# A transformer block pair on one core: quarter sums of weights by accumulating DMAs in DRAM, norm weights on the activations, seven products for the conv's output

## The chip, the core and the metric

The kernel runs on one core of a Trainium2 chip. The metric is the device time of one execution in microseconds: 2034.69 us, the median of three runs (2034.37 to 2036.16). A row such as L242 names line 242 of the kernel before; PE is TensorE, DVE VectorE, ACT ScalarE, POOL GpSimd, SP SyncE, whose queue carries the loads.

## What is computed

512 tokens of width 1024, all in fp32, in two blocks one behind the other.

```python
def first_block(x, ...):
    xn = rmsnorm(x, norm1_g)
    qa, ka, va, qr, kr, vr, gr, gate_a, gate_b = split(xn @ w_in)
    # dilated window attention (3 groups of 4 heads), retention (4 heads), gates, projections
    x = x + mix @ w_out
    return x + relu(rmsnorm(x, norm2_g) @ w_up) ** 2 @ w_down      # 1024 -> 4096 -> 1024
def second_block(x, ...):
    h = rmsnorm(x, a_norm)
    b, c, u, z = split(h @ a_w_in)                                  # 1024 -> 4 x 2048
    y = b * conv3(c * u) * silu(z)                                  # causal, 3 taps
    x = x + y @ a_w_out                                             # 2048 -> 1024
    # shared keys and values, then compressed, selected and window attention
    return rmsnorm(x, final_norm)
```

The rmsnorm is x / sqrt(mean(x^2) + 1e-6) * g; g are the norm weights.

## The kernel before

Every product is made of fp32r halves: each operand is split into hi (rounded, by ACT) and lo (the rest, by DVE), and `mm3` (L241 to L244) issues three matmuls, hi hi, hi lo and lo hi. A unit of weights is 512 rows by 512 columns, 1 MB; it costs 48 matmuls of 512 columns for all tokens. `Weights` (L42 to L158) keeps a list of all units in order: `get` (L151) hands out one, starts the load of the unit two further on (SP's queue, two raw buffers of 512 KB) and splits the next one. A unit without a norm weight is split in pieces of 128x1024 (ACT L127, DVE L128); one with a norm weight in four times as many instructions of 128x512, since the weight g goes with the row (ACT L131, DVE L132).

`gemm` (L267) takes two units of 1024 rows and accumulates four banks. With `halves` it takes the tokens 0 to 255 first and then 256 to 511, so that it can start when half of the activations are there.

The FFN's second product, `down(q)` (L808), is done by `gemm7` (L246) for each quarter q of the 4096: the quarter of activations and the 1024x1024 of weights are cut in 2 x 2 and multiplied with seven products instead of eight (Strassen's scheme, in Winograd's form). It needs sums of the activation parts (s1 to s4) and of the weight parts (t1 to t4). The weight parts w11, w12, w21, w22 are loaded, and DVE adds them in place between the splits (L118; splits L113, L114). The activation sums are made when `up` evacuates: ACT and DVE split them (`operand`, L765 and L766), DVE makes s1 (L793) and POOL s2, s3, s4 (L796, L797, L799). One product of `gemm7` is 24 matmuls of 512 columns (2 token tiles x 4 x 3). The order is p1 p5 p2 p3 p7 p6 p4; DVE adds the banks to the residual (L815), in the last quarter POOL adds u = p1 to six places of it.

At the end of the last `down` the rows are normed (`norm`, L226: ACT squares, DVE takes one-element steps L206 to L214 for the inverse root, and scales to xs, L235), transposed by PE (`split_T`, L216, PE L221) and split (ACT L223, DVE L224); then the conv's first `gemm` starts, in halves. The conv: `conv_blocks(j)` (L875), j = 0 to 3, makes 512 channels each in four `gemm`s c, u, z, b; `conv_out(j, cb)` (L923) multiplies them with a_w_out in plain products of 48 matmuls, 8 of them, and DVE adds half of the result to the residual (L929). Behind the last one the four tokens are normed and transposed one by one, for the keys and values of the attention (`kc_run`, L990, again in halves). The order of the jobs is that of the program; between products, generators of attention and retention issue their steps.

## Time and profile before

| | |
|---|---|
| median of 3 runs | 2034.69 us (2034.37 to 2036.16) |
| profiled execution | 2032.5 us, its span 2030.7 us |
| PE busy | 1981.3 us, 98% of the span, 9836 instructions |
| DVE busy | 1215.2 us, 60% |
| ACT busy | 912.8 us, 45% |
| POOL busy | 214.9 us, 11% |
| DMA | 185.75 MB, mean 91 GB/s |

Busy time is the sum over an engine's instructions. The profile's waits tell what released an engine that had been idle; its windows give busy time, granted clock and the share of the DMA engines for a stretch of the span.

### The profile page before, as it was taken

Reading aid. Unit: us, or ns where it says so; the run is one execution under the profiler, and the core shown is the slowest. Engines: PE = TensorE matmul, PEld = TensorE weight load, DVE = VectorE, ACT = ScalarE, POOL = GpSimd, SP = SyncE. Lnnn points to the kernel's source line nnn. Section 1 sums busy time; section 2 is a strip of 40 time slices with the busy share of each in tenths; the row PEclk is TensorE's granted clock in tenths of the full one; section 3 lists DMA queues with packets and bytes.
Section 4 is the critical chain, followed back from the end, with each engine's and each line's share of the span. In section 5 each row is a group of like instructions: output and inputs, shape, how many; then the busy total and the mean of one; then the engine's idle time right before and its main releaser. Section 6 shows DMA issues by size and latency. Waiting matters only on the chain. (4 is left out here: it accounts for less than half of the span.)

```text
span 2030.7 us, 25768 instructions
## 1 busy us (share of the span) xinstructions
PE 1981.3 (98%) x9836; PEld 1642.8 (81%) x9836; DVE 1215.2 (60%) x2183; ACT 912.8 (45%) x1723; POOL 214.9 (11%) x276
## 2 busy tenths in 40 slices
PE   8999999999999999999999899999999999999997
PEld 6888887888888888888888688888888898787776
DVE  6464456464555664486876955344435645769777
ACT  5454443333424233564453443333233334677776
POOL 0000001000000000011010301010101001315452
PEclk9999999999999999999999999999999999999999
DMA  4424322322223233413313133332332352210111
GB/s 152 145 68 125 95 68 84 102 70 88 84 88 94 79 96 127 157 62 124 114 63 125 31 94 91 97 103 84 104 104 83 124 164 84 63 52 28 67 32 42
DMA packets 104363, 185.75 MB, mean 91 GB/s; under 512 B 6896, under 2 KB 27920, under 8 KB 103984
## 3 DMA queue, kind: packets, MB, share of 16 engines
q1 hardware_dynamic: 99920, 172.51, 27.5%
q10 hardware_dynamic: 3264, 7.30, 1.0%
q0 software_dynamic: 1056, 4.29, 0.6%
q8 instruction: 77, 1.26, 0.3%
q14 instruction: 46, 0.38, 0.1%
HBM read 177.74 MB, written 6.34 MB: 91 GB/s over the span
## 5 line engine op out<-in xcount | busy, mean ns | idle before, releaser
L132 DVE SCALAR_TENSOR_TENSOR wl<-raw,vec,wh 128x512 fp32r<-128x512 f32 (+2 forms) x480 | 332.8, 730 | 311.8 <-ACT wh L131 300.7
L244 PE MATMUL g<-xh,wl 128*128 128x512 f32 (+1 forms) x1280 | 479.8, 375 | 2.9 <-DVE wl L132 2.9
L242 PE MATMUL g<-xh,wh 128*128 128x512 f32 (+1 forms) x1280 | 481.7, 377 | 0.6 <-ACT xh L223 0.6
L243 PE MATMUL g<-xl,wh 128*128 128x512 f32 (+1 forms) x1280 | 478.5, 374 | 0.0
L131 ACT ACTIVATE wh<-raw,vec 128x512 fp32r<-128x512 f32 (+2 forms) x480 | 309.4, 690 | 371.4 <-PE g L243 217.9
L244 PEld LDWEIGHTS g<-xh,wl 128*128 128x128 f32 x1280 | 241.5, 189 | 46.8 <-DVE wl L132 4.2
L242 PEld LDWEIGHTS g<-xh,wh 128*128 128x128 f32 x1280 | 241.5, 189 | 42.4 <-ACT xh L223 1.2
L243 PEld LDWEIGHTS g<-xl,wh 128*128 128x128 f32 x1280 | 241.7, 189 | 41.7 <-DVE xl L224 0.2
L242 PE MATMUL g<-wh,xh 128*128 128x512 f32 x512 | 204.4, 400 | 0.4 <-ACT wh L131 0.4
L243 PE MATMUL g<-wl,xh 128*128 128x512 f32 x512 | 201.4, 393 | 0.3 <-DVE wl L132 0.3
L244 PE MATMUL g<-wh,xl 128*128 128x512 f32 x512 | 200.7, 392 | 0.0
L242 PEld LDWEIGHTS g<-wh,xh 128*128 128x128 f32 x512 | 96.7, 189 | 20.1 <-ACT wh L131 1.1
L244 PEld LDWEIGHTS g<-wh,xl 128*128 128x128 f32 x512 | 96.4, 188 | 20.2 <-DVE xl L224 0.3
L243 PEld LDWEIGHTS g<-wl,xh 128*128 128x128 f32 x512 | 96.7, 189 | 18.8 <-DVE wl L132 0.7
L128 DVE TENSOR_TENSOR wl<-raw,wh 128x1024 fp32r<-128x1024 f32 x44 | 53.9, 1224 | 78.2 <-ACT wh L127 76.9
L127 ACT ACTIVATE wh<-raw 128x1024 fp32r<-128x1024 f32 (+1 forms) x60 | 56.5, 944 | 95.2 <-PE g L244 58.1
L796 POOL TENSOR_TENSOR s<-s,r 128x512 f32<-128x512 f32 x8 | 13.5, 1685 | 767.1 <-DVE s L793 767.1
L113 ACT ACTIVATE wh<-w 128x1024 fp32r<-128x1024 f32 x56 | 58.9, 1057 | 65.9 <-PE g L244 58.7
L114 DVE TENSOR_TENSOR wl<-w,wh 128x1024 fp32r<-128x1024 f32 x56 | 71.0, 1279 | 23.7 <-ACT wh L113 23.5
L1340 POOL TENSOR_TENSOR p<-p,ad 128x512 f32<-128x512 f32 (+3 forms) x96 | 68.3, 740 | 102.3 <-DVE ad L1335 97.8
L1328 ACT ACTIVATE p<-ps,am 128x512 f32<-128x512 f32 (+3 forms) x128 | 66.2, 529 | 22.4 <-DVE am L1326 17.1
L1326 DVE TENSOR_REDUCE am<-ps 128x1 f32<-128x512 f32 (+3 forms) x88 | 53.6, 637 | 17.3 <-PE ps L1324 16.4
(353 smaller groups left out, 3448.6 us busy)
## 6 DMA issues: line engine op xcount, KB each, us to landing
raw<-in_w_in SPq DMA_DIRECT2D x84, 512.0 KB, 3.6
raw<-in_a_w_in SPq DMA_DIRECT2D x64, 512.0 KB, 3.9
raw<-in_w_up SPq DMA_DIRECT2D x32, 512.0 KB, 4.0
w<-in_w_down SPq DMA_DIRECT2D x32, 512.0 KB, 4.2
raw<-in_w_in SPq DMA_DIRECT2D x32, 256.0 KB, 3.2
raw<-in_w_proj_b SPq DMA_DIRECT2D x16, 512.0 KB, 3.7
raw<-in_a_w_out SPq DMA_DIRECT2D x16, 512.0 KB, 3.9
raw<-in_b_w_in SPq DMA_DIRECT2D x16, 512.0 KB, 3.8
```

The costliest lines, as they stand in the source:

```text
L113: nc.scalar.activation(wh, raw, AF.Copy)
L114: nc.vector.tensor_sub(wl, raw, wh.bitcast(F32))
L127: nc.scalar.activation(wh[:, k], raw[:, k], AF.Copy)
L128: self.sub.tensor_sub(wl[:, k], raw[:, k], wh[:, k].bitcast(F32))
L131: nc.scalar.activation(wh[:, k], raw[:, k], AF.Copy, scale=gk)
L132: nc.vector.scalar_tensor_tensor(wl[:, k], raw[:, k], gk, wh[:, k].bitcast(F32), op0=ALU.mult, op1=ALU.subtract)
L242: PE.matmul(ps, lh, rh, start=start, stop=False, skip_group_check=not check)
L243: PE.matmul(ps, lh, rl, start=False, stop=False, skip_group_check=not check)
L244: PE.matmul(ps, ll, rh, start=False, stop=stop, skip_group_check=not check)
L1326: V.tensor_reduce(m[:, h0:h0 + hp], ps, axis=AX.X, op=ALU.max, negate=True)
L1328: A.activation(p[:, h], ps[:, h], AF.Exp, bias=m[:, h0 + h:h0 + h + 1], accum_out=d[:, h0 + h:h0 + h + 1])
L1340: G.tensor_tensor(pp[h], pp[h], d[:, h:h + 1].to_broadcast([P, n]), op=ALU.mult)
```

## The change

Five things are done together.

- Quarter sums. t1 to t4 of the four `down` quarters and of the two 1024x1024 blocks of a_w_out are formed in DRAM: POOL issues a copy DMA of a quarter and then a DMA that adds another quarter to it. For each of the six blocks these are four copies and four adds of 1 MB, 48 DMAs in all. They are issued four at a time, behind a one-column copy on POOL that reads a result of the retention's q/k, gate and v products (`sum_some`). The seven units of a block are then loaded like any others.
- Raw buffers are four instead of two until the attention stage begins.
- The norm weights of norm1, norm2 and anorm are multiplied onto the activations in `split_T` (eight pieces of 128x128 a token tile, each with its scale), so that the units of w_in, w_up and a_w_in are split in pieces of 128x1024. Two norms keep theirs on the weights.
- `gemm7` runs in the order p1 p7 p4 p5 p6 p2 p3; all activation sums are made on DVE, s3 with a11 in the first pass. In the last block, tokens 256 to 511 are normed after p6 and tokens 0 to 255 after p3; the next `gemm` takes the half of tokens 256 to 511 first, then come the transposes of the others (`late`), then the other half.
- The conv's output product is two `gemm7`s, one before the b product of block 2 and one at the end. The factor 0.5 goes into the taps.

The diff, cut to its core:

```diff
-    ORDER = ("w11", "t1", "w21", "w22", "t3", "t2", "t4")
...
+    def raws_in(self, pool, bufs):
+        while self.raws:
+            self._split()
+        self.raw_pool, self.raw_bufs = pool, bufs
...
-            raw = self.pool.tile([128, 1024], F32, tag="raw", name="raw", bufs=2)
+            raw = self.raw_pool.tile([128, 1024], F32, tag="raw", name="raw", bufs=self.raw_bufs)
...
-        if isinstance(raws, str):
-            for raw in self.q[self.PLACE.get(raws, raws)]:
-                wh, wl = self._halves(2, 512)
-                nc.scalar.activation(wh, raw, AF.Copy)
-                nc.vector.tensor_sub(wl, raw, wh.bitcast(F32))
-                out += [(wh[:, k], wl[:, k]) for k in range(2)]
-            for a, b in self.SUMS.get(raws, ()):
-                for x, y in zip(self.q[a], self.q[b]):
-                    nc.vector.tensor_tensor(x, x, y, op=ALU.add)
-            self.ready.append(out)
-            return
...
-    def split_T(dst_h, dst_l, t, src):
+    def split_T(dst_h, dst_l, t, src, gain=None):
         for b in range(2):
             ps = psa.tile([P, 4, P], F32, tag="tr", name="tr", bufs=2)
             for k in range(4):
                 PE.transpose(ps[:, k], src[:, (4 * b + k) * P:(4 * b + k + 1) * P], ident)
             oh = dst_h[:, 4 * b:4 * b + 4, t * P:(t + 1) * P]
-            A.activation(oh, ps, AF.Copy)
-            V.tensor_sub(dst_l[:, 4 * b:4 * b + 4, t * P:(t + 1) * P], ps, oh.bitcast(F32))
+            ol = dst_l[:, 4 * b:4 * b + 4, t * P:(t + 1) * P]
+            if gain is None:
+                A.activation(oh, ps, AF.Copy)
+                V.tensor_sub(ol, ps, oh.bitcast(F32))
+            else:
+                for k in range(4):
+                    gk = vcol(gain, 4 * b + k, 4 * b + k + 1)
+                    A.activation(oh[:, k], ps[:, k], AF.Copy, scale=gk)
+                    V.scalar_tensor_tensor(ol[:, k], ps[:, k], gk, oh[:, k].bitcast(F32),
+                                           op0=ALU.mult, op1=ALU.subtract)
...
+    late = []
+    def arrive(t, xs, gain=None):
+        x = cur["x"]
+        if t < 2:
+            late.append(lambda: split_T(*x, t, xs, gain))
+        else:
+            split_T(*x, t, xs, gain)
...
-        for name, o, base in (("p1", "a11", None), ("p5", "s1", None), ("p2", "a12", "p1"), ("p3", "s4", "p5"),
-                              ("p7", "s3", None), ("p6", "s2", None), ("p4", "a22", "p7")):
+        for name, o, at_ in (("p1", "a11", "g0"), ("p7", "s3", "g1"), ("p4", "a22", "g1"), ("p5", "s1", "os"),
+                             ("p6", "s2", "g1"), ("p2", "a12", "g0"), ("p3", "s4", "os")):
             w = ws.get()
-            bb = banks[name] = banks[base] if base else [psg.tile([P, 512], F32, tag="g", name="g") for _ in range(2)]
+            new = name in ("p1", "p7", "p5", "p6")
+            if new:
+                banks[at_] = [psa.tile([P, 512], F32, tag=at_[i], name="g") if at_ == "os" else
+                              psg.tile([P, 512], F32, tag="g", name="g") for i in range(2)]
...
+    def st_unit(w, k0, c0, sums):
+        d = {f"w{a + 1}{b + 1}": (w, k0 + 512 * a, 4, [(c0 + 512 * b, 512)], None) for a in range(2) for b in range(2)}
+        d.update({n: (sums[n], 0, 4, [(0, 512)], None) for n in sums})
+        return [d[n] for n in ("w11", "t3", "t4", "t1", "t2", "w21", "w22")]
+    def st_sums(w, k0, c0):
+        q = {(a, b): w[k0 + 512 * a:k0 + 512 * a + 512, c0 + 512 * b:c0 + 512 * b + 512]
+             for a in range(2) for b in range(2)}
+        t = {n: dr.tile([512, 512], F32, name=f"{n}_{len(st_names)}") for n in ("t1", "t2", "t3", "t4")}
+        st_names.append(0)
+        def put(n, src):
+            return lambda: G.dma_start(out=t[n], in_=src)
+        def add(n, src):
+            return lambda: G.dma_start(out=t[n], in_=src, accum_op=ALU.add)
+        return t, [put("t1", q[0, 0]), put("t3", q[0, 1]), add("t1", q[0, 1]), add("t3", q[1, 1]),
+                   put("t2", t["t1"]), add("t2", q[1, 1]), put("t4", t["t2"]), add("t4", q[1, 0])]
+    def operands(make, hold, first, h, r0, r1, scratch):
+        def put(name, src):
+            if h == 0:
+                hold[name] = [make(name, x) for x in "hl"]
+            hi, lo = (x[:, 2 * h:2 * h + 2] for x in hold[name])
+            A.activation(hi, src, AF.Copy)
+            V.tensor_sub(lo, src, hi.bitcast(F32))
+        a11, a21 = r0[:, :, 0:256], r0[:, :, 256:512]
+        if first:
+            put("a11", a11)
+            s3 = scratch()
+            V.tensor_sub(s3, a11, a21)
+            put("s3", s3)
+            return
+        a12, a22 = r1[:, :, 0:256], r1[:, :, 256:512]
+        s1, s2 = scratch(), scratch()
+        put("a22", a22)
+        V.tensor_sub(s1, a21, a22)
+        put("s1", s1)
+        V.tensor_sub(s2, s1, a11)
+        put("s2", s2)
+        put("a12", a12)
+        V.tensor_tensor(s2, s2, a12, op=ALU.add)
+        put("s4", s2)
+    def acc7(u, first, last, done, before=False):
+        res = cur["res"]
+        lo, hi = slice(0, 512), slice(512, 1024)
+        def add(dst, ps, op=ALU.add):
+            V.tensor_tensor(dst, dst, ps, op=op)
+        def add_u(i, u):
+            add(res[:, 2 + i, hi], u, ALU.subtract)
+            add(res[:, 2 + i, lo], u)
+            add(res[:, i, hi], u, ALU.subtract)
+        def evac(name, i, ps):
+            if name == "p1" and (first or last):
+                A.activation(u[:, i], ps, AF.Copy)
+            elif name == "p1":
+                add(u[:, i], ps)
+            elif name == "p6" and not last:
+                add(u[:, i], ps)
+                if before:
+                    add_u(i, u[:, i])
+            elif name == "p6":
+                add_u(i, ps)
+                done(2 + i)
+            elif name == "p7":
+                add(res[:, 2 + i, hi], ps, ALU.subtract)
+            else:
+                t, cols = {"p5": (2, hi), "p2": (0, lo), "p3": (0, hi), "p4": (2, lo)}[name]
+                add(res[:, t + i, cols], ps)
+                if last and name == "p4":
+                    add_u(i, u[:, i])
+                if last and name == "p3":
+                    done(i)
+        return evac
...
+        order = {"first": (0, 1), "last": (1, 0), None: (0,)}[halves]
+        for q in order:
+            if halves == "last" and q == 0:
+                while late:
+                    late.pop(0)()
...
+    sums = {}
+    for q in range(4):
+        sums["down", q], steps_ = st_sums(I["w_down"][0], q * 1024, 0)
+        sum_steps.extend(steps_)
+    for m in range(2):
+        sums["out", m], steps_ = st_sums(I["a_w_out_2"][0], m * 1024, 0)
+        sum_steps.extend(steps_)
+    def sum_some(n, after):
+        if sum_steps:
+            tiny = st.tile([P, 1], F32, tag="tiny", name="tiny")
+            guard = G.tensor_copy(tiny, after[:, 0:1])
+            with tc.issue_after(guard.ins):
+                for _ in range(min(n, len(sum_steps))):
+                    sum_steps.popleft()()
...
+            sum_some(4, hi[:, 0].bitcast(F32))
...
         def run():
+            def done(t):
+                if t == 2:
+                    cur["x"] = new_x()
+                if t == 2:
+                    ff["xs"] = fft("xs", (P, 2, D), "r0", 1)
+                xs = ff["xs"][:, t - 2] if t > 1 else fft("xs", (P, D), "r1", 2)
+                norm(cur["res"][:, t], xs, ff["r2"][:, t:t + 1])
+                arrive(t, xs, "anorm")
+                V.tensor_scalar(cur["res"][:, t], cur["res"][:, t], ff["r2"][:, t:t + 1], None, op0=ALU.mult)
+            gemm7(lambda name: ff[q][name], acc7(ff["u"], q == 0, q == 3, done, q == 2))
+        job(st_unit(I["w_down"][0], q * 1024, 0, sums["down", q]), run)
...
+            gemm(False, xk, 2, lambda i, ps: A.activation(cv["c", j][:, i], ps, AF.Copy),
+                 halves="last" if j == 0 else None)
...
+            if o == 0 and j == 2:
+                conv_out(0)
+            job(U(a_in, 0, 8, [(o + j * 512, 512)]), fn)
...
+    def conv_out(m):
         def run():
-            hi, lo = cv["y", j]
-            def evac(t, ps):
-                dst = cur["res"][:, t, cb * 512:(cb + 1) * 512]
-                V.scalar_tensor_tensor(dst, ps, 0.5, dst, op0=ALU.mult, op1=ALU.add)
-                if j == 3 and cb == 1:
-                    if t == 0:
-                        cur["x"] = new_x()
-                    norm_T(*cur["x"], t, cur["res"][:, t], cv["p"].tile([P, D], F32, tag="xs", name="xs", bufs=2))
-                    nc.scalar.dma_start(out=hdram[t * P:(t + 1) * P, :], in_=cur["res"][:, t])
-            gemm(True, lambda k: (hi[:, k], lo[:, k]), 1, evac)
-        job(U(a_out, j * 512, 4, [(cb * 512, 512)]), run)
-    conv_blocks(0)
+            def done(t):
+                if t == 2:
+                    cur["x"] = new_x()
+                if t % 2 == 0:
+                    cv["xs"] = cv["p"].tile([P, 2, D], F32, tag="c", name="xs", bufs=3)
+                norm(cur["res"][:, t], cv["xs"][:, t % 2])
+                arrive(t, cv["xs"][:, t % 2])
+                nc.scalar.dma_start(out=hdram[t * P:(t + 1) * P, :], in_=cur["res"][:, t])
+            gemm7(lambda name: cv["y", m][name], acc7(cv["u"], m == 0, m == 1, done, m == 0))
+        job(st_unit(a_out, m * 1024, 0, sums["out", m]), run)
     for j in range(4):
-        if j < 3:
-            conv_blocks(j + 1)
-        conv_out(j, 0), conv_out(j, 1)
+        conv_blocks(j)
+    conv_out(1)
...
+        ws.raws_in(None, 2)
...
+        gemm(False, xk, 2, evac, halves="last")
```

How the instructions are moved, at three places. First TensorE at the end of the last `down`, where the conv's first product starts (a and s are operands of the seven products, xs normed rows, xh and xl their split transposes). Before:

```order
L242 MATMUL g<-wh,a_8599 128x512
L243 MATMUL g<-wl,a_8599 128x512
L244 MATMUL g<-wh,a_8600 128x512
L221 MATMUL tr<-ident,xs 128x128 x16
L242 MATMUL g<-xh,wh 128x256 x4
L243 MATMUL g<-xl,wh 128x256
L244 MATMUL g<-xh,wl 128x256
```

All sixteen transposes of the first two token tiles stand behind the last product, p4. Now:

```order
L219 MATMUL g<-wh,s_8555 128x512
L184 MATMUL tr<-ident,xs 128x128 x8
L220 MATMUL g<-wl,s_8555 128x512
L221 MATMUL g<-wh,s_8556 128x512
L184 MATMUL tr<-ident,xs 128x128 x8
L219 MATMUL g<-xh,wh 128x256
L220 MATMUL g<-xl,wh 128x256
L221 MATMUL g<-xh,wl 128x256
```

Eight transposes stand two matmuls ahead of the end of the last product, p3, and eight behind it. Later, between the two halves of the conv's first product:

```order
L219 MATMUL g<-xh,wh 128x256
L220 MATMUL g<-xl,wh 128x256
L221 MATMUL g<-xh,wl 128x256
L184 MATMUL tr<-ident,xs 128x128 x16
L219 MATMUL g<-xh,wh 128x256 x4
```

Before, the transposes of the last two token tiles stood in three lots among the matmuls of the first half. The end of the conv has the same rows in the changed kernel.

Second, VectorE in that place, between the last additions to the residual (L305 in the changed kernel) and the split of the transposes (L194), where L91 is the split of the weights and L206 makes xs:

```order
L91 TENSOR_TENSOR wl<-raw,wh 128x1024
L177 SCALAR_TENSOR_TENSOR rstd<-rs_a,rstd 128x1
L173 SCALAR_TENSOR_TENSOR rs_a<-rstd,msq 128x1
L205 TENSOR_TENSOR rstd<-rstd,r_6362 128x1
L305 TENSOR_TENSOR res<-res,g 128x512
L206 TENSOR_SCALAR xs<-res,rstd 128x1024
L177 SCALAR_TENSOR_TENSOR rstd<-rs_a,rstd 128x1
L890 TENSOR_SCALAR res<-res,r_6362 128x1024
L173 SCALAR_TENSOR_TENSOR rs_a<-rstd,msq 128x1
L91 TENSOR_TENSOR wl<-raw,wh 128x1024
L194 SCALAR_TENSOR_TENSOR xl<-tr,vec,xh 128x128 x2
```

The steps of the norms now stand among the additions of p2 and p3 and among five weight splits; before, they stood behind p6 and p4.

Third, POOL's queue from the attention's last instruction on. Before:

```order
L499 TENSOR_TENSOR o<-o,w_96 128x512 x4
L796 TENSOR_TENSOR s_6748<-s_6747,r_6391 128x512
L797 TENSOR_TENSOR s_6749<-r_6391 128x512
L799 TENSOR_TENSOR s_6748<-s_6748,r_6730 128x512
L796 TENSOR_TENSOR s_6808<-s_6807,r_6391 128x512
```

Behind the merge of the attention groups stand the activation sums of the FFN.

Now (t_0_98 and its like are the sums in DRAM; L262 copies, L265 adds):

```order
L570 TENSOR_TENSOR o<-o,w_96 128x512 x4
L632 COPY tiny<-rk 128x1
L262 DMA t_0_98<-in_w_down 512x512
L262 DMA t_0_100<-in_w_down 512x512
L265 DMA t_0_98<-in_w_down 512x512
L265 DMA t_0_100<-in_w_down 512x512
L632 COPY tiny<-o 128x1
L262 DMA t_0_99<-t_0_98 16x16384
L265 DMA t_0_99<-in_w_down 512x512
L262 DMA t_0_101<-t_0_99 16x16384
L265 DMA t_0_101<-in_w_down 512x512
```

The sums of the activations are gone from POOL, and six times these ten rows stand there, one half for each of twelve products of the retention; the guards read the pages rk, o and tk in turn.

## Rows read from the trace of the kernel before

**Rows 1.** The page: busy time by engine, and the granted clock in 40 slices.

```profile
PE 1981.3 (98%) x9836; PEld 1642.8 (81%) x9836; DVE 1215.2 (60%) x2183; ACT 912.8 (45%) x1723; POOL 214.9 (11%) x276
...
PEclk9999999999999999999999999999999999999999
```

**Rows 2.** TensorE's waits: line, waited for, us in total, times, longest.

```profile
PE tr L221 <- DVE msq L230: 3.9, 2, 3.7
...
PE g L244 <- DVE wl L132: 2.9, 3, 1.0
...
PE g L242 <- ACT s L765: 2.1, 1, 2.1
PE g L244 <- DVE s L766: 2.0, 1, 2.0
```

**Rows 3.** Windows: length, then busy by engine (count), PEclk, DMA share, GB/s.

```profile
350.00:770.00 420.00, 420.00 (x1912) 349.01 (x1911) 231.06 (x458) 148.47 (x227) 0.00 (x0) 1.00 0.28 87
870.00:1120.00 250.00, 247.06 (x1088) 203.54 (x1087) 189.50 (x207) 129.27 (x183) 30.61 (x19) 1.00 0.30 97
1124.00:1148.00 24.00, 18.05 (x65) 13.24 (x64) 22.77 (x22) 10.35 (x14) 15.87 (x9) 0.86 0.10 29
1166.00:1178.00 12.00, 7.19 (x42) 6.33 (x41) 11.87 (x40) 6.75 (x12) 0.00 (x0) 0.72 0.42 126
1350.00:1600.00 250.00, 250.00 (x1095) 205.33 (x1094) 113.96 (x156) 78.14 (x112) 11.84 (x14) 1.00 0.32 97
1600.00:1624.00 24.00, 23.54 (x127) 19.35 (x126) 18.13 (x57) 11.37 (x20) 0.00 (x0) 1.00 0.39 138
```

Busy times are in the order PE, PEld (weight load), DVE, ACT, POOL.

**Rows 4.** Conv's output product: one of its lines, and two evacuations (start, us).

```profile
L242 PE MATMUL g<-wh,yh 128*128 128x512 f32 x128 | 50.6, 395 | 0.0
...
1588.44 0.69 DVE L929 SCALAR_TENSOR_TENSOR res<-g,res 128x512 f32<-128x512 f32 x1 [2.11 <-PE g L244]
1591.24 0.69 DVE L929 SCALAR_TENSOR_TENSOR res<-g,res 128x512 f32<-128x512 f32 x1 [2.11 <-PE g L244]
```

**Rows 5.** TensorE's timeline in p7 of the last `down`, twenty matmuls apart.

```profile
1149.31 0.39 PE L243 MATMUL g<-wl,s 128*128 128x512 f32 x1
...
1153.85 0.39 PE L242 MATMUL g<-wh,s 128*128 128x512 f32 x1
```

**Rows 6.** DVE by line and form: count | busy us, mean ns | idle before.

```profile
L132 DVE SCALAR_TENSOR_TENSOR wl<-raw,vec,wh 128x512 fp32r<-128x512 f32 x424 | 306.5, 760 | 302.4 <-ACT wh L131 291.8 <-PE g L244 10.3
...
L815 DVE TENSOR_TENSOR res<-res,g 128x512 f32<-128x512 f32 x46 | 30.8, 682 | 6.9 <-PE g L244 6.1 <-POOL res L815 0.6
...
L210 DVE SCALAR_TENSOR_TENSOR rs_a<-rstd,msq 128x1 f32<-128x1 f32 x36 | 7.6, 216 | 0.5
...
L235 DVE TENSOR_SCALAR xs<-res,rstd 128x1024 f32<-128x1024 f32 x8 | 6.0, 748 | 0.0
```

**Rows 7.** DVE's timeline in the last `down`: weight splits beside POOL, and without.

```profile
1134.09 4.53 DVE L114 TENSOR_TENSOR wl<-w,wh 128x1024 fp32r<-128x1024 f32 x2
...
1149.70 1.23 DVE L114 TENSOR_TENSOR wl<-w,wh 128x1024 fp32r<-128x1024 f32 x1 [0.16 <-ACT wh L113]
```

**Rows 8.** POOL's timeline in the same place.

```profile
1132.34 10.92 POOL L815 TENSOR_TENSOR res<-res,u 128x512 f32<-128x512 f32 x6
```

**Rows 9.** DMA issues: count, KB each, median us from issue to landing.

```profile
raw<-in_a_w_out SPq DMA_DIRECT2D x16, 512.0 KB, 3.9
...
v<-vdram POOLq DMA_DIRECT2D x2, 1024.0 KB, 5.8
...
w<-in_cmp_w_v SPq DMA_DIRECT2D x2, 1024.0 KB, 9.5
```

**Rows 10.** Pages rk and tk of the retention: first writes (DVE), last writes (ACT).

```profile
L554 DVE TENSOR_TENSOR rk<-g,rk x16: 678/684/692, 326.7 to 635.5; 128x512 fp32r<-128x512 f32 x16
...
725.30 0.58 ACT L686 ACTIVATE rk<-g 128x512 f32<-128x512 f32 x1
...
738.82 0.63 ACT L705 ACTIVATE tk<-rk 128x512 fp32r<-128x512 f32 x1 [3.53 <-DVE rk L704]
```

More of the change, by code (lines that the diff above doesn't have):

```diff
@@ L272, in gemm @@
+    def gemm(xs_mode, xk, nu, evac, pace=1, halves=None):
         banks = [psg.tile([P, 512], F32, tag="g", name="g") for _ in range(4)]
         ww = [ws.get() for _ in range(nu)] if halves else None
-        for q in range(2 if halves else 1):
+        order = {"first": (0, 1), "last": (1, 0), None: (0,)}[halves]
[3 more added lines that the diff above has]
+                    late.pop(0)()
             cols = slice(256 * q, 256 * q + 256) if halves else slice(0, 512)
@@ L301, in U @@
                 for u in range(0, nk, per)]
-    def st_unit(w, k0, c0):
-        return [("st", w, k0, c0, what) for what in Weights.ORDER]
     xp = ctx.enter_context(tc.tile_pool(name="xp", bufs=1))
@@ L368, in run @@
             gemm(True, xk, 2, evac, 2)
-        job(U(w_in, 0, 8, [(col + g * 512, 512)], "norm1"), run)
+        job(U(w_in, 0, 8, [(col + g * 512, 512)]), run)
     def v_block(g):
@@ L389, in run @@
             bg.append(attn(g))
-        job(U(w_in, 0, 8, [(3072 + g * 512, 512)], "norm1"), run)
+        job(U(w_in, 0, 8, [(3072 + g * 512, 512)]), run)
     def s2(shape, name, dt=F32):
@@ L534, in run @@
             gemm(False, xk, 2, lambda i, ps: A.activation(y[:, i], ps, AF.Tanh, scale=0.5), 2)
-        job(U(w_in, 0, 8, [(10752 + cb * 512, 512)], "norm1"), run)
+        job(U(w_in, 0, 8, [(10752 + cb * 512, 512)]), run)
     def proj_a(cb):
@@ L568, in run @@
             gemm(True, xk, 2, lambda i, ps: split2(hi[:, i], lo[:, i], ps))
+            sum_some(4, hi[:, 0].bitcast(F32))
             rt["gen", h] = ret(h)
             bg.append(rt["gen", h])
-        job(U(w_in, 0, 8, [(6656 + h * 512, 512)], "norm1"), run)
+        job(U(w_in, 0, 8, [(6656 + h * 512, 512)]), run)
     def ret(h):
@@ L645, in run @@
             rt["sg", h] = sg
-        job(U(w_in, 0, 8, [(8704 + h * 512, 512)], "norm1"), run)
+            sum_some(4, sg[:, 0])
+        job(U(w_in, 0, 8, [(8704 + h * 512, 512)]), run)
     def proj_b(h):
@@ L694, in run @@
             gemm(False, xk, 2, evac)
-        job(U(w_in, 0, 8, [(11776 + cb * 512, 512)], "norm1"), run)
+        job(U(w_in, 0, 8, [(11776 + cb * 512, 512)]), run)
     def blend(cb, i, t):
```

190 lines of the change are left out of this document (54 added, 136 removed).

## The prediction

> **What bounds the kernel now.** I read the page first, then TensorE's waits, then the table of windows by stage, then the timelines of the two or three windows that were not full. The page shows TensorE busy 1981.3 of 2030.7 us and its clock at 9 tenths or more in every slice [rows 1]: TensorE is the bound, and only two things can change the time, the matmuls themselves and the 49 us in which it idles. The waits of TensorE [rows 2] are few and short, and the windows [rows 3] say where they lie. In the retention stage (350 to 770 us) and in the conv's stage (1350 to 1600) PE is busy all the time; from 870 to 1120 it loses 2.9 us. The one bad place is the end of the FFN: from 1124 to 1148 PE works 18.05 of 24 us at clock 0.86, and from 1166 to 1178, where the conv starts, 7.19 of 12 us at 0.72. The end of the conv (1600 to 1624) loses only 0.46 us. The reader is to see that DVE is busy 22.77 and 11.87 us in those two windows: there DVE, not TensorE, sets the pace.
>
> **Part 1, the conv's output product.** Before, it is 8 products of 48 matmuls, 128 on each of three lines (one of them in [rows 4]), so 384; the change issues 2 x 7 products of 24, so 336. Two evacuations of this product, 12 matmuls apart, lie 2.80 us apart [rows 4], which is 0.2333 us for a matmul. The seven products of the FFN run faster: twenty matmuls in 4.54 us [rows 5], 0.2267 each, and 24 in 5.44 us. Nothing else is done there, so the gain is 48 x 0.2333 = 11.2 us if the spacing stays, and 384 x 0.2333 - 336 x 0.2267 = 13.4 us if it becomes that of the FFN's products. I take the middle, **-12.3 us**.
>
> **Part 2, the end of the FFN.** What it costs now: 24 - 18.05 = 5.95 us idle and 18.05 x 0.14 = 2.5 us by the clock in the first window, 12 - 7.19 = 4.81 and 7.19 x 0.28 = 2.0 in the second, together 15.3 us [rows 3]. In the first window the waits are for s, made by ACT and DVE (2.1 and 2.0 us), and then for the split of the weights [rows 2]. That split is slow there: two L114 take 4.53 us beside POOL's six additions of 10.92 us, and one alone takes 1.23 us a little later [rows 7, 8]. The change takes all of this off POOL and the weight sums off DVE, and asks for s3 and a11 a whole product earlier, so p1 to p3 run through: the 8.5 us of the first window go to zero.
>
> The second window keeps its kind. Now p6 comes before p2 and p3, so the norms of tokens 2 and 3 have 2 x 5.44 = 10.9 us of cover, and the first half of the conv's product uses only these two. What DVE has to do in that time, by the order of the changed kernel: 6 additions (0.68 us each), 2 xs and one scaling of res (0.75), some 14 one-element steps (0.2) [rows 6], 5 weight splits (1.23) [rows 7], and 8 pieces of 128x128 of the new split with the gain. For such a piece there is no row: it lies between a one-element step (0.22) and a 128x512 addition (0.68), nearer the first by its length, and I take 0.28. That is 4.1 + 2.25 + 2.8 + 6.15 + 2.2 = 17.5 us in durations; instructions back to back overlap a little, so about 16.5. PE waits some 5.5 us for the last transposes. The sixteen late transposes of tokens 0 and 1 then stand between the halves, and their pieces cost ACT and DVE another 2 us of waiting. The clock after an idle stretch of that length falls as it did at 1166, 2 to 2.5 us. Sum 10 us in place of 15.3: **-5.3 us**, with ends -13 (cover suffices) and 0 (DVE still late as before).
>
> **Part 3, the end of the conv.** Before, the four tokens came one by one out of a plain product, and the transposes hid behind it, 0.46 us of idling [rows 3]. Now the same end as above stands here: p6, the additions, two norms, transposes, half of the next product. DVE's list between p6 and the first half is 7 additions, one split of 1.23 us, 5 splits of 128x512 (0.76), 16 small steps, 2 xs and 4 copies of 128x512, 16 to 17 us against the same 10.9 us of cover; without the gain's 8 pieces on ACT and without the scaling of res it is a little lighter. I take 4 us of waiting, 1 at the late transposes and 2 by the clock, less the 0.5 of before: **+6.5 us**, ends +1 and +9.
>
> **Part 4, gains on the activations.** The splits of w_in, w_up and a_w_in go from two DVE instructions of 128x512 (0.76 us each) [rows 6] to one of 128x1024 (1.23) [rows 7], and ACT saves likewise. In the stages with a full PE this buys nothing: a split runs beside 48 matmuls and is done in time. Only the 2.9 us of waits for L132 [rows 2], all in the FFN [rows 3], go: **-2.9 us** (ends 0 and -2.9). At the start the norm's pieces are more and shorter; ends -0.5 and +1.5, I take **+0.5**.
>
> **Part 5, the sums in DRAM.** 24 copies and 24 accumulating copies of 1 MB on POOL's queue, four at a time behind a small copy. POOL does nothing between 350 and 770 [rows 3], so it can wait there; the cost is either in the weight loads or in the guard. No row shows a transfer from DRAM to DRAM or one that adds. The nearest: 1 MB from DRAM on POOL's queue lands in 5.8 us, 1 MB beside others on SP's in 9.5 [rows 9]; a sum reads two and writes one, so three times the first, 17 us, is the other end. 48 MB one after the other take 280 to 820 us at most and two run side by side; the first sums are needed at about 870, the conv's after 1400. SP's loads of 512 KB land in 3.9 us [rows 9] and DMA is 0.28 busy there [rows 3]; a 1 MB unit is eaten in 10.9 us (48 matmuls), and the loads run more than a unit ahead. I take **0** from both ends; what it costs without that cover is the third rival. The Trainium skill (DMA: Bandwidth & Descriptors, Anatomy of one DMA, SWDGE path) puts such a transfer at 2.0 us plus its bytes over 436 GB/s, which is 4.4 us as an estimate for 1 MB; the row has 5.8 and decides. By 4.4 us the sum would be the same and the third rival would be gone; by 17 us it decides the case.
>
> **Sum.** -12.3 - 5.3 + 6.5 - 2.9 + 0.5 = -13.5 us on the profiled 2032.5 us: 2019.0. The median of the runs, 2034.69, is 2.2 us above that execution, so the forecast is **2021 us**. 0.2% is 4 us, about what a measurement of this kernel can tell from none, so faster ends at 2030.6 and slower begins at 2038.8.
>
> **Rivals.**
> 1. *Both ends run through.* If the two norms fit behind p2 and p3, part 2 is -13, part 3 is +1: 2021 - 7.7 - 5.5 = 2008 us. For it: DVE's list misses the cover by a third only. Against: DVE was busy 11.87 of 12 us there [rows 3].
> 2. *Both ends bound by DVE.* The POOL additions that the change hands to DVE, and the pieces of the split at twice my price (16 per two tokens on two engines), leave part 2 at 0 and make part 3 +12: 2034.7 - 12.3 - 2.9 + 0.5 + 12 = 2032 us. For it: no cover was ever shown for that chain at the conv's end. Against: p1 to p3 lose a cause that is plain in [rows 7, 8].
> 3. *POOL's queue falls behind; slower.* Each unit of sums has five links one behind the other (put, add, put, add, put; the last add runs beside the next put), and the guard that reads a page of the retention stands behind them. The last guard comes after 5 x 5 + 1 = 26 links from about 340 us (the first evacuation starts at 326.7 [rows 10]), and the page that it reads is written again at 738.8 [rows 10]. It decides when a link takes over (739 - 340) / 26 = 15.3 us. At 17 us the write waits until 782: +43 us, 2064 us. Against: 5.8 and 9.5 us [rows 9]. The Trainium skill (SBUF — State Buffer, SBUF: two separate sides) says that POOL cannot write descriptors while certain DVE instructions hold the shared ports; no run here shows it, and it would make a link longer.
> 4. *Loads bound the seven products.* A seven-product unit now loads 7 MB in 38 us where four were loaded, and each product of 5.44 us needs its two loads of 3.9 us [rows 5, 9]. If a load landed 0.5 us too late for each of the 42 products: +21, 2042 us. Against: four raw buffers, and DMA far from full in every window [rows 3].
> 5. *Spacing.* The same matmul runs at 0.2333 us [rows 4] and at 0.2267 [rows 5], and nothing in the trace says why. The change moves tiles about; if the plain products of 350 to 770 and 870 to 1120 took the slower one, 670 us x 2.9% = +20, 2041 us. Equally the last products may keep it, which is in part 1's bounds.
>
> **How the numbers follow.** The forecast, with its own range of 2010 to 2030, has 0.61; rival 1 0.08, rival 2 0.12 (a third of it faster, the rest within 0.2%), rival 3 0.07, rival 4 0.06, rival 5 0.06. Faster: 0.61 + 0.08 + 0.04 = 0.73; the same 0.08; slower 0.07 + 0.06 + 0.06 = 0.19. The range reaches from rival 1's 2008, less 1 for part 1, to 2036, which takes in rival 2 with its spread and leaves out the three slower ones.
>
> **What would show it.** Part 1: 336 matmuls with the conv's operands at 0.227 to 0.233 us. Part 2: the waits for s and for the split before p3's end gone, clock 1.0 up to the last product; then one wait of 5 to 6 us at the transposes, with a dip of the clock, and a short one between the halves. Part 3: the same picture at the end of the conv, where there was none. Part 4: no PE wait on a weight split in the FFN. Part 5: PE still full from 350 to 770, POOL waiting on its own transfers, SP's loads landing within 5 us. Wrong would be: PE idle on a page or on a weight in the retention stage (rivals 3 and 4), fewer matmuls in 420 full us of the retention than the 1912 of before [rows 3] (rival 5), or waits over 10 us at either end (rival 2).

## The result, and the profile after

The changed kernel takes 2055.12 us (median of 4 runs, 2052.76 to 2058.84) beside 2035.4 us for the kernel before on the same chip: a ratio of 1.0099, 95% interval 1.0081 to 1.0116. It is 20 us slower where 14 us faster were forecast, and it lies outside the range. The profiled execution has a span of 2051.0 us. In this and the following sections all executions have a mean granted clock of 0.99 or more of TensorE's full speed; the one exception, an execution of e1 at 0.655 that took 2809.7 us, is left out of e1's numbers.

Windows of the changed kernel, columns as in [rows 3] (length, then PE, PEld, DVE, ACT, POOL with their counts, PEclk, DMA share, GB/s):

```profile
350.00:770.00 420.00, 420.00 (x1871) 341.80 (x1870) 222.47 (x407) 131.65 (x174) 37.51 (x55) 1.00 0.76 199
870.00:1120.00 250.00, 250.00 (x1074) 201.18 (x1073) 151.26 (x181) 123.63 (x159) 0.00 (x0) 1.00 0.45 139
...
1180.00:1190.00 10.00, 4.89 (x25) 4.47 (x24) 9.94 (x39) 6.76 (x20) 0.00 (x0) 0.66 0.37 114
...
1200.00:1210.00 10.00, 7.24 (x51) 6.99 (x50) 5.52 (x17) 5.49 (x16) 0.13 (x2) 0.83 0.00 0
```

The first line is the result. PE is as full as before and its clock is 1.00, yet it starts 1871 instructions in the 420 us where it started 1912 [rows 3]. TensorE does not wait; its matmuls follow each other more slowly. In the second line the sums can be no reason, since the last of them is issued at 714 us. This line is full as well, where before 2.94 us of it were idle, and yet it has 1074 instructions instead of 1088. The third and fourth lines are the FFN's end, where the clock dips as before.

TensorE's timeline in a product of the FFN, eighteen matmuls apart:

```profile
951.76 0.39 PE L219 MATMUL g<-xh,wh 128*128 128x512 f32 x1
...
955.96 0.39 PE L219 MATMUL g<-xh,wh 128*128 128x512 f32 x1
```

That is 4.20 us for 18, 0.2333 us each. Before, the conv's output had this spacing [rows 4] and the FFN's products had 0.2267 [rows 5]. The same holds over the whole trace: in every stretch of 200 us, neighbouring matmuls of 512 columns lie 0.232 to 0.234 us apart on average, where before it was 0.227 to 0.228 up to the end of the conv.

TensorE's waits in the changed kernel (line, waited for, us, times, longest):

```profile
PE tr L184 <- DVE rstd L177: 9.2, 1, 9.2
PE tr L184 <- DVE xl L194: 7.9, 2, 5.1
```

The first line is the start of the kernel (before, 9.3 us). The waits for s and for L132 of [rows 2] are gone, as forecast; what replaced them is the second line, one wait of 5.1 us at the FFN's end and one of 2.8 between the halves. The new transfers, and the weight load beside them that lands later than before (count, KB, median us to landing):

```profile
t<-in_w_down POOLq DMA_DIRECT2D x24, 1024.0 KB, 11.5
...
raw<-in_w_proj_b SPq DMA_DIRECT2D x16, 512.0 KB, 6.2
...
t<-t POOLq DMA_DIRECT2D x12, 7.2
```

So parts 2 and 4 look as they should, and so does TensorE's side of part 5; but the loads of w_proj_b on SP's queue land in 6.2 us at the median (before, 3.7), where "within 5 us" was the sign. Over everything lies the slower spacing.

### The profile page after: what moved, and what is told of

Same layout as the page of the kernel before. It is cut to its first block, busy times and chain, and to the rows that moved or that the text cites. A ratio compares the mean times of both kernels' runs of the same rounds, so it can differ in the third digit from the quotient of the medians.

```text
span 2051.0 us, 25691 instructions
## 1 busy us (share of the span) xinstructions
PE 2005.5 (98%) x9788; PEld 1636.7 (80%) x9788; DVE 1184.5 (58%) x2114; ACT 898.1 (44%) x1633; POOL 202.7 (10%) x306
## 3 DMA queue, kind: packets, MB, share of 16 engines
q0 software_dynamic: 17376, 54.63, 11.2%
## 5 line engine op out<-in xcount | busy, mean ns | idle before, releaser
L91 DVE TENSOR_TENSOR wl<-raw,wh 128x1024 fp32r<-128x1024 f32 (+1 forms) x312 | 377.4, 1213 | 431.4 <-ACT wh L90 430.6
L90 ACT ACTIVATE wh<-raw 128x1024 fp32r<-128x1024 f32 (+1 forms) x328 | 335.9, 1028 | 493.6 <-PE g L220 227.7
L219 PE MATMUL g<-xh,wh 128*128 128x512 f32 (+1 forms) x1280 | 487.1, 382 | 0.5 <-ACT xh L188 0.4
L220 PE MATMUL g<-xl,wh 128*128 128x512 f32 (+1 forms) x1280 | 485.0, 380 | 0.0
L220 PE MATMUL g<-wl,s 128*128 128x512 f32 x192 | 76.1, 396 | 0.0
L1373 ACT ACTIVATE p<-ps,am 128x512 f32<-128x512 f32 (+3 forms) x128 | 66.1, 528 | 22.4 <-DVE am L1371 16.7
L219 PE MATMUL g<-wh,s 128*128 128x512 f32 x192 | 75.9, 396 | 0.0
L221 PE MATMUL g<-wh,s 128*128 128x512 f32 x192 | 75.9, 395 | 0.0
L95 DVE SCALAR_TENSOR_TENSOR wl<-raw,vec,wh 128x256 fp32r<-128x256 f32 (+2 forms) x88 | 49.5, 595 | 24.9 <-ACT wh L94 24.6
L1371 DVE TENSOR_REDUCE am<-ps 128x1 f32<-128x512 f32 (+3 forms) x88 | 53.5, 636 | 17.5 <-PE ps L1369 16.7
## 6 DMA issues: line engine op xcount, KB each, us to landing
t<-in_w_down POOLq DMA_DIRECT2D x24, 1024.0 KB, 11.5
```

What stands on the lines that cost most here:

```text
L90: nc.scalar.activation(wh[:, k], raw[:, k], AF.Copy)
L91: self.sub.tensor_sub(wl[:, k], raw[:, k], wh[:, k].bitcast(F32))
L95: nc.vector.scalar_tensor_tensor(wl[:, k], raw[:, k], gk, wh[:, k].bitcast(F32), op0=ALU.mult, op1=ALU.subtract)
L219: PE.matmul(ps, lh, rh, start=start, stop=False, skip_group_check=not check)
L220: PE.matmul(ps, lh, rl, start=False, stop=False, skip_group_check=not check)
L221: PE.matmul(ps, ll, rh, start=False, stop=stop, skip_group_check=not check)
```

## What else moved: the addresses

Rival 5 said that the same matmul has two spacings and that nothing in the trace says why. The trace has no addresses; the compiled programs have. These are the addresses, within a partition, of the first buffer of the products' operands (in both programs, all buffers of a name have the same remainder modulo 256):

```
                      before               changed kernel
weight split wh       27520  mod 256: 128  19328   128
activations xh        62592           128  54528     0
conv's output yh     136384           192  (seven products' operands: 0)
```

Before, 6920 of the 7304 matmuls with 512 columns have both operands at remainder 128. The other 384 are those of the conv's output, with 128 against 192: the slow ones of [rows 4]. In the changed kernel the raw buffers have left the pool of the weight splits, which shifts what comes behind by 8192 bytes, a multiple of 256; and the guard's one-column tile (`tiny`) stands in a small pool between the weight splits and everything else, with four buffers of 32 bytes. Those 128 bytes leave wh at 128 and put nearly every other operand at 0, so that 6888 of 7256 matmuls with 512 columns have operands 128 bytes apart.

**Theory 1:** a matmul of 512 columns takes 0.2267 us where its two SBUF operands have the same address modulo 256, and some 0.006 us more otherwise. **Rival A:** something else in the change (the traffic of the sums, the order of the banks, the raw pool) slows TensorE. **Theory 2** says that the sums are hidden behind TensorE's work, **rival B** that their traffic is paid for. **Theory 3** says that the end of the conv gives back what its second block of seven products saves.

## The experiments

**e1: the changed kernel with the addresses put back.**

```diff
-            tiny = st.tile([P, 1], F32, tag="tiny", name="tiny")
+            tiny = st.tile([P, 1], F32, tag="tiny", name="tiny", bufs=8)
```

> The changed kernel, with 8 instead of 4 buffers for the guard's one-column tile: it takes 256 bytes of each partition instead of 128, so that activations and weight splits, which lay 128 bytes apart modulo 256 in the changed kernel, have the same remainder again, as they had before. Theory 1 (address): a matmul of 512 columns takes 0.2267 us when its two SBUF operands have the same address modulo 256 and 0.2325 to 0.2333 otherwise; then all 7256 such matmuls become faster by 0.006, the spacing is 0.2267 in every stage and the time falls by 30 us or more, to about 2020 us (2012 to 2026). Rival A (the accumulating DMAs, the bank order of the seven products or the raw pool slow TensorE): nothing changes, 2055 us within 3.

Measured: 2022.8 to 2024.5 us, ratio to the kernel before 0.9945 (0.9929 to 0.9962). Four more buffers of a tile that nobody reads take 31 us off. With them the change is faster than the kernel before; without them it was slower by the 128 bytes.

**e2: the kernel before with the shift.**

```diff
+    space = st.tile([P, 32], F32, tag="space", name="space", bufs=1)
+    G.memset(space, 0.0)
     ident = cp.tile([P, P], F32, name="ident")
```

> The kernel before, with an unused tile of 128 bytes ahead of the activations and behind the weight splits (and one memset of it): the only other change is the address of everything behind it. Theory 1: spacing 0.2325 to 0.2333 in every stage, about 2068 us (2060 to 2076). Rival A: 2035 us, spacing 0.2267.

Measured: 2067.04 us, ratio 1.0157 (1.0142 to 1.0172), +32.7 us. The window of the retention in its profile:

```profile
350.00:770.00 420.00, 420.00 (x1870) 341.89 (x1869) 230.13 (x457) 146.46 (x226) 0.00 (x0) 1.00 0.27 85
```

1870 instructions, close to the changed kernel's 1871, with no sum and with DMA at 0.27. Rival A falls. One stage is not at the forecast spacing of 0.2325 to 0.2333: the shift puts the conv's output operands 64 bytes away from the weights instead of 192. Two evacuations of that product, 12 matmuls apart:

```profile
1619.41 0.69 DVE L931 SCALAR_TENSOR_TENSOR res<-g,res 128x512 f32<-128x512 f32 x1 [2.05 <-PE g L246]
1622.15 0.69 DVE L931 SCALAR_TENSOR_TENSOR res<-g,res 128x512 f32<-128x512 f32 x1 [2.06 <-PE g L246]
```

That is 2.74 us, or 0.228 a matmul, between the 2.80 of [rows 4] and the 2.72 that e4 has at equal remainders. The map m1 gives the same order for 64 bytes.

**e3: the kernel before, both operands shifted.** The same two lines, with the tile in the pool `cp` ahead of the weight splits.

> The kernel before, with an unused tile of 128 bytes ahead of both, weight splits and activations: both move by 128, so that their difference stays 0 and their remainder modulo 256 goes from 128 to 0. Theory 1 in the form that the difference counts: 2035 us, spacing 0.2267. Theory 1 in the form that the remainder itself counts (128 is good, others are not): about 2068 us, spacing 0.2325 to 0.2333.

Measured: 2035.02 us, ratio 1.0001 (0.9991 to 1.0011). Its window:

```profile
350.00:770.00 420.00, 420.00 (x1912) 349.27 (x1911) 231.09 (x458) 147.96 (x227) 0.00 (x0) 1.00 0.28 87
```

1912, as before. With remainder 0 on both sides nothing is lost: it is the difference that counts.

**e4: the conv's output operands aligned.**

```diff
-                vp_ = cv["p"].tile([P, S + 2], F32, tag="vp", name="vp", bufs=2)
+                vp_ = cv["p"].tile([P, S + 32], F32, tag="vp", name="vp", bufs=2)[:, :S + 2]
```

> The kernel before, with 30 columns more in the conv's padded tile, so that the conv's output operands (remainder 192 before) get the remainder 128 of the weight splits. Theory 1: the 384 matmuls of the conv's output go from 0.2333 to 0.2267 us, 2.6 us less, 2032 to 2033 us; all else as before. Rival A: no change, 0.2333.

Measured: 2031.81 us, ratio 0.9989 (0.998 to 0.9998). Two evacuations of the product, 12 matmuls apart (DVE's timeline; compare [rows 4]):

```profile
1588.07 0.69 DVE L929 SCALAR_TENSOR_TENSOR res<-g,res 128x512 f32<-128x512 f32 x1 [2.03 <-PE g L244]
1590.79 0.69 DVE L929 SCALAR_TENSOR_TENSOR res<-g,res 128x512 f32<-128x512 f32 x1 [2.03 <-PE g L244]
```

2.72 us instead of 2.80, 0.2267 a matmul. The time agrees with the expected 2.6 us but lies at the edge of what it can tell from none; the rows settle it.

**m1: a map of the addresses.** Not the model: groups of 48 matmuls with different starts, each closed by a copy of its bank on DVE.

```diff
+    def group(md, wds, n=48):
+        b = ps.tile([P, 512], F32, tag="g", name="g")
+        for i in range(n):
+            e = wds[i % len(wds)] + 128 * (i // len(wds) % 4)
+            PE.matmul(b, w[:, e:e + 128], m[:, md:md + 512], start=i == 0, stop=i == n - 1)
+        V.tensor_copy(acc[:, 0:512], b)
```

> Not the model: 32 groups of 48 matmuls (fp32r, 128x128 by 512 columns), each group with another start of the moving or of the stationary operand, nothing else; the output is not the reference's. A group at 0.2267 us each takes 10.9 us, at 0.2333 11.2 us. Theory 1: 10.9 wherever the difference of the two starts is a multiple of 256 bytes, 11.2 at 64, 128 and 192 bytes; what holds at 16, 32 and 240 bytes, and when the stationary operands alternate between a good and a bad start, is open: if the load of the next stationary operand beside the running matmul is what collides, an alternating group lies between the two.

The copies of DVE's timeline; the time from one to the next is that of a group:

```profile
175.81 0.69 DVE L182 COPY acc<-g 128x512 f32<-128x512 f32 x1 [10.51 <-PE g L181]
186.72 0.69 DVE L182 COPY acc<-g 128x512 f32<-128x512 f32 x1 [10.21 <-PE g L181]
197.91 0.69 DVE L182 COPY acc<-g 128x512 f32<-128x512 f32 x1 [10.50 <-PE g L181]
208.81 0.69 DVE L182 COPY acc<-g 128x512 f32<-128x512 f32 x1 [10.20 <-PE g L181]
...
385.22 0.69 DVE L182 COPY acc<-g 128x512 f32<-128x512 f32 x1 [10.21 <-PE g L181]
396.41 0.69 DVE L182 COPY acc<-g 128x512 f32<-128x512 f32 x1 [10.50 <-PE g L181]
...
418.65 0.69 DVE L182 COPY acc<-g 128x512 f32<-128x512 f32 x1 [10.39 <-PE g L181]
429.70 0.69 DVE L182 COPY acc<-g 128x512 f32<-128x512 f32 x1 [10.36 <-PE g L181]
440.58 0.69 DVE L182 COPY acc<-g 128x512 f32<-128x512 f32 x1 [10.19 <-PE g L181]
```

Each group has its own distance between the two operands. The first four rows are the groups whose moving operand starts 240, 256, 384 and 512 bytes behind the stationary one: 10.91 us at 256, 11.19 at 384, 10.90 at 512. By the moving operand's distance, modulo 256:

| bytes | 0 | 16 | 32 | 64 | 128 | 192 | 240 |
|---|---|---|---|---|---|---|---|
| us for 48 | 10.88 | 11.12 | 11.20 | 10.99 | 11.16 | 11.20 | 11.19 |

At 64 bytes 11.2 was expected; 10.99 is a miss of theory 1 in its simple form, since that distance costs only a third. When the stationary operand is moved instead, 64, 128 and 192 bytes give 11.20, 11.16 and 10.99: the same, with the sign turned. At 16 bytes the two ways differ (moving the stationary one by 16 gives 10.89, by 240 10.97), so the turned sign holds for the multiples of 32 that were tried, not below. Both moved alike: 10.88 to 10.90. The group that ends at 396.41 alternates good and bad stationary operands and takes 11.19, as if all were bad; that ending at 429.70, with one bad in four, takes 11.05, somewhat over half of the way. It is as if a bad operand cost its own matmul and a neighbour. The expectation had one guess for the cause, that the load of the next stationary operand collides with the running matmul, and its sign was an alternating group between the two. That sign did not come, and no row shows such a load being late. Why the distance matters stays open.

**e5: e1 once more, for the profile.** The code is that of e1.

> The kernel of e1_guard_tile_256 once more, for a profile at full clock. Theory 1: spacing 0.2267 us in every stage, 2024 us within 3; the rest of the difference to before then lies in the terms of the prediction, and the profile shows which: conv's output 13.4 us less, no wait on a weight split in the FFN (2.9 less), the FFN's end some 3 us less and the conv's end some 3 us more. If the sums in DRAM cost something, PE shows idle time or a spacing above 0.2267 between 330 and 720 us, and only there.

Measured: 2021.77 us, ratio 0.9933 (0.9916 to 0.9949). Windows of its profile:

```profile
330.00:720.00 390.00, 390.00 (x1776) 324.16 (x1776) 205.64 (x385) 120.62 (x159) 41.64 (x57) 1.00 0.82 215
...
350.00:770.00 420.00, 420.00 (x1911) 349.06 (x1911) 223.60 (x409) 133.83 (x176) 39.53 (x55) 1.00 0.75 199
...
1124.00:1148.00 24.00, 24.00 (x107) 19.88 (x107) 23.36 (x36) 11.76 (x14) 0.00 (x0) 1.00 0.61 198
1148.00:1166.00 18.00, 13.04 (x66) 11.17 (x66) 17.77 (x62) 10.58 (x24) 0.00 (x0) 0.81 0.48 146
...
1165.00:1190.00 25.00, 22.23 (x176) 21.99 (x175) 10.97 (x28) 8.68 (x21) 0.13 (x2) 0.93 0.02 4
```

1911 instructions again in the 420 us. PE is full over the whole time of the sums, with DMA 0.82 busy, and starts as many instructions there as in the kernel before, whose line for the first window is:

```profile
330.00:720.00 390.00, 390.00 (x1775) 324.20 (x1774) 212.86 (x433) 134.29 (x207) 0.00 (x0) 1.00 0.28 86
```

So in this kernel the sums take nothing from TensorE. This profile is the one on which the prediction's terms can be read, and the next section does so.

**e6: the sums alone.** The kernel before, with the 48 DMAs at the places of the change and a guard tile of 256 bytes; nobody reads the sums.

```diff
+        tiny = st.tile([P, 1], F32, tag="tiny", name="tiny", bufs=8)
+        guard = G.tensor_copy(tiny, after[:, 0:1])
+        with tc.issue_after(guard.ins):
+            for _ in range(n):
+                sum_steps.popleft()()
...
             gemm(False, xk, 2, lambda i, ps: split2(hi[:, i], lo[:, i], ps))
+            sum_some(4, hi[:, 0].bitcast(F32))
```

> The kernel before with the 48 copy and accumulating DMAs of the change, at the same places of the retention (guard tile of 256 bytes, so that the addresses keep their remainders); nothing reads the sums. Theory 2 (the sums are hidden): 2034 us within 2. Rival B (their 100 MB of traffic slows loads or TensorE): 5 us or more above that, between 330 and 720 us.

Measured: 2038.62 us, ratio 1.0023 (1.0012 to 1.0034), +4 us. Window, then the wait in it:

```profile
330.00:720.00 390.00, 386.12 (x1747) 320.27 (x1746) 211.17 (x431) 132.76 (x206) 39.56 (x57) 1.00 0.82 214
...
PE s L242 <- DVE p L617: 3.9, 2, 2.3
```

So the sums are not free everywhere; the time lies between what theory 2 and rival B expected. PE loses 3.9 us in two waits for p, the retention's scores times the decay table. After the first of them the granted clock is 0.86 from 484 to 496 us, which costs some 2 us more. The chain behind the first wait (ACT, DVE, DVE, PE):

```profile
484.97 1.06 ACT L127 ACTIVATE wh<-raw 128x1024 fp32r<-128x1024 f32 x1 [2.61 <-DMA raw<-in_w_proj_b]
486.06 1.23 DVE L128 TENSOR_TENSOR wl<-raw,wh 128x1024 fp32r<-128x1024 f32 x1 [2.33 <-ACT wh L127]
487.21 0.68 DVE L617 TENSOR_TENSOR p<-s,dec 128x512 f32<-128x512 f32 x1
487.94 0.45 PE L242 MATMUL s<-rk 128*128 128x384 f32 x1 [2.31 <-DVE p L617]
```

A load of weights lands late, ACT waits for it to split it, DVE waits for ACT, and p stands behind that split on DVE. In the window ACT waits 36.8 us for loads of w_proj_b (nine times), where in the kernel before it waits for none; they land in 8.5 us at the median, before in 3.7. The decay table lands later too (9.2 us at the median and 15.4 at most, before 4.1 and 5.5), but it is not what p waits for: the table of this p is issued at 417.8 us and lands by 434, 53 us before it is used.

**e8: e6 with three raw buffers.**

```diff
-            raw = self.pool.tile([128, 1024], F32, tag="raw", name="raw", bufs=2)
+            raw = self.raw_pool.tile([128, 1024], F32, tag="raw", name="raw", bufs=self.raw_bufs)
...
+    ws.raws_in(pa, 3)
```

> The kernel of e6_before_sums_alone, with three raw weight buffers of 512 KB instead of two up to the FFN (other addresses keep their remainders). Theory 2 (the 4 us of e6 come from loads that queue behind weight loads with too little lead: PE waits on dec, the retention's decay table): the waits on dec go, 2034 to 2036 us. Rival B (the traffic of the sums slows TensorE or the loads whatever the lead): 2038 to 2040 us as in e6.

Measured: 2035.82 us, ratio 1.0005 (0.9996 to 1.0014). Its window:

```profile
330.00:720.00 390.00, 390.00 (x1776) 324.21 (x1775) 212.80 (x433) 134.32 (x207) 39.02 (x57) 1.00 0.81 215
```

The waits on p are gone, with the same traffic. The expectation had the number right and the load wrong: the decay table lands as late as in e6 (9.3 and 15.2 us at most) and does no harm, as there. What the third buffer changes is the weights. They are asked for earlier, so that although w_proj_b still takes 6.9 us to land, ACT no longer waits for it (0.6 us in the whole window). Of the two splits at the place shown above, the first waits for PE and the second, the one that was late in e6, for nothing:

```profile
477.43 1.06 ACT L133 ACTIVATE wh<-raw 128x1024 fp32r<-128x1024 f32 x1 [0.76 <-PE g L250]
...
479.28 1.06 ACT L133 ACTIVATE wh<-raw 128x1024 fp32r<-128x1024 f32 x1
```

So more raw buffers hide the sums. That the changed kernel, with its four, would pay without them was not run; it is argued from e6.

**e7: the second block of the conv's output as plain products.** e1, with `conv_out(1)` replaced by four plain products of 48, tokens normed and transposed one by one, the next product starting with tokens 0 to 255, and eight sum DMAs fewer.

```diff
-    conv_out(1)
+    for j in (2, 3):
+        conv_plain(j, 0), conv_plain(j, 1)
...
-        gemm(False, xk, 2, evac, halves="last")
+        gemm(False, xk, 2, evac, halves="first")
```

> The kernel of e1_guard_tile_256, with the second of the two seven-product blocks of the conv's output undone: channels 1024 to 2047 go through four plain products of 48 matmuls again, the tokens are normed and transposed one by one behind the last of them, and the attention's first product takes tokens 0 to 255 first, as before; eight sum DMAs less. Theory 3 (the end of the conv gives back what its second block saves): 24 matmuls more cost 5.4 us and the 8 us that PE loses at the conv's end fall to 0.5, so 2019 to 2022 us, 2 us under e5_guard_tile_256_again or the same within the noise; the profile has under 1 us of PE waiting between the last conv product and the compressed keys. Rival (the loss at the conv's end belongs to the attention's start, not to the order of the products): 2027 us, and the waits stay.

Measured: 2020.50 us, ratio 0.9931 (0.9918 to 0.9943), the same as e5 within the intervals. The first of the matmuls that compress the keys starts at 1634.0 us, in e5 at 1633.6: 24 matmuls more, and the end of the conv costs that much less. TensorE's waits there were 2.3, 1.0, 1.0 and 0.3 us in e5; here one of size is left, where under 1 us in all was expected:

```profile
PE g L219 <- ACT ev L1075: 1.5, 1, 1.5
```

Theory 3 holds in the time: the second block's seven products save 24 matmuls, 5.4 us, and their end gives about as much back. Of the versions measured this and e1 are the fastest, both faster than both kernels.

## Why the prediction was wrong

**The step that failed** is the one that put the spacing of the untouched products into the sum as fixed, a cost of nothing. I had seen that 384 matmuls were slower than the FFN's for no visible reason [rows 4, 5], and I let the change move every tile of the kernel. That is rival 5; I gave it 6 in 100 and costed it on two stages only: +20 us, 2041. It was all stages: 31 us (e1 against the changed kernel), 32.7 (e2). The view that would have told it was at hand: the one product with another spacing is the one whose operand has another remainder, and both kernels' addresses were fixed before any run.

Once the addresses are put back, the sum comes out near, and in part by luck, since its errors have both signs. Its terms, read in e5 against the kernel before at the same places of the program (start of the named operation in each profile):

| up to | before | e5 | the step itself | forecast |
|---|---|---|---|---|
| last addition of w_out (L721, L812) | 824.1 | 826.6 | +2.5 | +0.5 (start) |
| first evacuation of the conv's u (L887, L932) | 1214.0 | 1206.3 | -10.2 | -5.3 - 2.9 |
| last evacuation of its b (L914, L958) | 1572.5 | 1557.6 | -7.2 | -6.2 (half of -12.3) |
| first compression of keys (L1022, L1067) | 1646.9 | 1633.6 | +1.6 | +6.5 - 6.2 |
| end of the span | 2030.7 | 2021.2 | +3.8 | 0 |

- **The start.** +2.5 lies outside my ends (-0.5 and +1.5). After 20 us PE has started 33 instructions in e5 and 42 before; which of the shorter pieces costs it is not broken down.
- **Part 1.** In e5 the spacing became that of the FFN's products, so 384 x 0.2333 - 336 x 0.2267 = 13.4 us, the upper end; I took the middle for want of the cause. Half of it, 6.7 us, lies in the third step's -7.2.
- **Part 2.** p1 to p3 run through (24.00 of 24 us from 1124 to 1148), and the wait for the last transposes is 4.96 us, 5.5 forecast. The late transposes wait 2.77 us (2 forecast), because their two banks come free only after eight small pieces that ACT and DVE take in turn (3.15 us). Without part 4's 2.9 us the step gained 7.3 where 5.3 stood. Of this, 3.0 us are idle time (10.76 before, 7.73 in e5); the rest, the clock among it, is not broken down. The two waits in TensorE's timeline:

```profile
1160.16 1.97 PE L184 MATMUL tr<-ident,xs 128*128 128x128 f32 x8 [4.96 <-DVE xl L194]
...
1178.60 1.97 PE L184 MATMUL tr<-ident,xs 128*128 128x128 f32 x8 [2.77 <-DVE xl L194]
```

- **Part 3.** +1.6 with 6.7 saved in it is 8.3 us lost, 6.5 forecast. That this is near is luck. I had 4 us of waiting at the first transposes and 1 at the late ones; these waits are 1.3 and 1.0. Not in my list was a third, of 2.3 us: a weight split whose load stands behind loads of 1 MB that the attention's start puts ahead of it on SP's queue (L1029 issues two at 1614.5 us, the split's load follows at 1618.5). Part of the rest goes with the clock, 0.91 from 1615 to 1635 us; I had 2 us for it. ACT's timeline in e5:

```profile
1627.92 1.34 ACT L94 ACTIVATE wh<-raw,vec 128x512 fp32r<-128x512 f32 x2 [2.20 <-DMA raw<-in_b_w_in]
```

- **Part 4.** No PE wait on a split is left in the FFN, as forecast.
- **Part 5.** Nothing, as forecast for this kernel; but my reason (POOL idle, DMA mostly idle, loads more than a unit ahead) was not enough: e6 and e8 show that with two raw buffers the loads come too late. A copy lands in 4.8 to 16.7 us, where I had 5.8 to 17, and loads of w_proj_b in 9.4, where I had all of SP's within 5. Rival 3 stayed away: in the changed kernel the last guard runs at 685 us, and the page that it reads (tk) is written again at 754.6.
- The attention, which the change does not touch, is 3.8 us longer in this profile. Kernels without the change differ there by 3 us too (383.7 to 386.8 us from the first compression to the end), so no cause is claimed for it.

Together this is 11 to 14 us faster by the ratios of e1 and e5 (0.9945 and 0.9933), against the 13.5 of the sum.

What the Trainium skill states for a transfer of this kind (DMA: Bandwidth & Descriptors, Anatomy of one DMA, SWDGE path: 4.4 us as an estimate for 1 MB) lies under the rows here: 7.2 us for a copy within DRAM and 11.5 for the transfers that read w_down, with the weight loads beside them. The measurements decide; the sum did not hang on it.

## What to carry to other kernels

Before a change is timed, compare the addresses of both matmul operands modulo 256 with those of the kernel before: a small tile in a pool between them shifts everything behind it, and 1.6% of this TensorE-bound kernel's time hung on 128 bytes (e2). Two spacings of one instruction form in a profile are a question to be answered first, since every estimate for untouched work rests on it. A gain at a boundary is to be counted with the end that it creates: seven products saved 5.4 us in the last block and cost as much where the next stage had been fed token by token. And a wait is to be followed to its end: TensorE waited for p, and behind p stood a late load of weights.

## What the runs showed of the hardware that was not expected

- fp32r matmuls of 128x128 by 512 columns follow each other at 0.2267 us when the two SBUF operands start at the same address modulo 256 bytes, and at 0.229 (64 bytes), 0.2325 (128) or 0.2333 (192, 32) when the moving one lies that much behind (m1; in the model e2 has 128 and 64, e3 and e4 have 0). One bad stationary operand in four costs about as much as two slow matmuls in four. This is read where such matmuls stand in long rows; in the attention, among small ones, neighbours lie 0.23 us apart at equal remainders too.
- A copy of 1 MB within DRAM on POOL's queue landed in 7.2 us beside other traffic, and 48 transfers in some 390 us, half of them adding, took nothing from TensorE (e5, e8), though they about doubled the landing time of loads on SP's queue (256 KB: from 4.1 to 9.4 us, e5). With two raw buffers that was enough to make TensorE wait (e6).
